# Feed-forward middle tiles: TensorE transposes replaced by VectorE 32x32 block transposes and a trip through DRAM

## The chip, the cores and the metric

The kernel runs on one core of one Trainium2 chip. The metric is the device time of one execution in microseconds (us). The engines are TensorE (PE, with its weight loads as PEld), VectorE (DVE), ScalarE (ACT), GpSimd (POOL) and SyncE (SP), which here issues every DMA.

## The reference

The program is a transformer-like network on a sequence of 256 tokens with 1024 channels: two layers of (feed-forward, mixer, feed-forward), then one mixer, one cross attention and a last feed-forward. There are five feed-forwards, all of one shape. Only they are changed:

```python
def swiglu_ffn(h, w_in, w_out):
    gate, up = jnp.split(h @ w_in, 2, axis=-1)
    return (jax.nn.silu(gate) * up) @ w_out
```

The middle has 2816 channels (`D_FF`), so `w_in` is 1024 x 5632 and `w_out` is 2816 x 1024. All of it is float32.

## The kernel before

The 256 tokens are two tiles of 128 (`t` = 0, 1). Every float32 product is made of three products in a shorter format: an operand is split into a high part (ScalarE's cast to `fp32r`) and a low part (VectorE's difference), and `mac` (L266 to L270) issues high x high (L268), high x low and low x high on TensorE.

Weights stream from DRAM in tiles of 128 x 1024 floats (512 KB) by `wload` (L157 to L166). Each passes three stations. SP loads it into one of `NS` = 5 places of the ring `stage` (L99), ScalarE casts it into one of `NW` = 4 places of `whi` (L164), and VectorE writes the difference into one of 4 places of `wlo` (L165). A load must wait until VectorE has finished with the tile five earlier, a cast until TensorE has finished with the tile four earlier.

`ffn` (L351 to L375) goes over the 2816 middle channels in six chunks, five of 512 and one of 256. A chunk takes four weight tiles for the gate and four for the up half, each tile 12 matmuls; the last chunk has both halves in four tiles. The products come out token-major, tokens on the 128 partitions. For each token tile ScalarE takes the silu (`sg`, L366) and VectorE multiplies it with the up half (`hb`, L368). The second product contracts over the middle channels, so `hb` must be turned: channels on the partitions. `to_T` (L257 to L264) does it with one TensorE transpose per 128 x 128 block, four per token tile, into a PSUM tile `tp` (L262). `split_evac` then reads `tp` twice, once for ScalarE's high part `hTh` (L187) and once for VectorE's low part `hTl` (L188). After the six chunks `lin_out` multiplies `hTh` and `hTl` with 22 tiles of `w_out`, starting with channel block 0.

The order on each engine is set at build time by a scheduler that simulates the program, with priorities: weight loads, casts and differences run ahead of the rest. On the chip each engine then takes its instructions strictly in that order, and so does SP with its DMAs. In the second layer's second feed-forward a preparation of the next block (`s5_prelude`) is put behind chunk 1, and it fills VectorE.

Of the kernel before, what the change touches and what calls it, by code (L numbers as in the profile page):

```python
# [8 lines left out]
F32 = mybir.dt.float32  # L9
# [3 lines left out]
ALU = mybir.AluOpType  # L13
# [3 lines left out]
P = 128  # L17
# [12 lines left out]
ASIDE = 1  # L30
BANKS = dict(mm=7, ch=3, tp=3, chs=4, tpm=2, mmm=3)
BUFS = dict(
    sg=2, hb=2,
    cg=2, xb=2, gv=2, gu=2, sq=2, q=2, k=2, kv=4, xs=2, xd=2, y=2, yo=2, jk=2, pr=2, pT0=2, pT1=2, ao=2, L=2, cbm=2, rp=2,
    D1=2, Mb=2, pm=2, XT=2, X=3, s5m0=2, s5x0=2, s5t=4, sq2=2, tg=1, o2=1, vn=2)
SEQ = "x u q z S A g0 b0 g2 g1 b2 b1"
# [2 lines left out]
LAST = ((0, 512), (512, 256), (768, 256))  # L39
# [13 lines left out]
class Arena:  # L53


    def __init__(self, net, n, name):
        self.t, self.at = net.A([n], name), 0
# [9 lines left out]
class Net:  # L67
    def __init__(self, ctx, tc, a, outs):
        self.tc, self.nc, self.a, self.outs = tc, tc.nc, a, outs
        mk = lambda n, b=None, **k: ctx.enter_context(tc.tile_pool(name=n, bufs=b, **k))  # L70
        self.big = mk("big")
        self.sma, self.small = None, {}
        self.junk = mk("junk", 1)
        self.ps = mk("ps", space=PSUM)
        self.lane = ""
        self.wdma, self.ahead = [], []
        self.sma = Arena(self, 1536, "small")
        self.stage = self.A([NS, 1024], "stage")
        self.whi, self.wlo = [self.A([NW, 1024], n, F32R) for n in ("whi", "wlo")]
        nc = self.nc  # L80
        self.cst = Arena(self, 1024, "cst")
        self.triu = self.load(self.cst, a["c_triu"], [P, P], "triu")
        self.cmask = self.load(self.cst, a["c_cmask"], [P, P], "cmask")
        self.rowm = self.load(self.cst, a["c_rowm"], [P, 4], "rowm")
        self.ones = self.cst.tile([P, P])
        nc.vector.memset(self.ones, 1.0)
        self.mhalf = self.cst.tile([P, 8])
        nc.vector.memset(self.mhalf, -0.5)
        self.euler = self.cst.tile([P, 16])
        nc.vector.memset(self.euler, math.e)  # L90
        self.x = [self.A([D], f"x{t}") for t in range(2)]
# [48 lines left out]
    def mm(self):  # L140
        return self.bank("mm")
# [115 lines left out]
    def to_T(self, src, n, hi, lo, t):  # L257
# [3 lines left out]
        for k in range(n):  # L261
            nc.tensor.transpose(p[:, k * P:(k + 1) * P], src[:, k * P:(k + 1) * P], self.ident)  # L262
        self.split_evac(self._shape(p[:, :n * P], [n, P]),
                        hi[:, :, t * P:(t + 1) * P], lo[:, :, t * P:(t + 1) * P])  # L264

    def mac(self, out, lh, ll, rh, rl, first, last):  # L266
        mm = self.nc.tensor.matmul
        mm(out, lh, rh, start=first, stop=False)  # L268
        mm(out, lh, rl, start=False, stop=False)  # L269
        mm(out, ll, rh, start=False, stop=last)  # L270
# [80 lines left out]
    def ffn(self, norm, w_in, w_out, scale, nxt, aside=None):  # L351
        nc = self.nc
        xT, r = norm["xT"], norm["r"]
        hh, hl = [], []
        for c in range(6):
            n = 512 if c < 5 else 256
            th = self.A([4, S], "hTh", F32R)
            tl = self.A([4, S], "hTl", F32R)
            ps = self.lin_tok(xT, w_in[c * 8:c * 8 + 4], 512)
            if c < 5:  # L360
                pg, pu = ps, self.lin_tok(xT, w_in[c * 8 + 4:c * 8 + 8], 512)
            else:
                pg, pu = [[p[:, i * n:(i + 1) * n] for p in ps] for i in range(2)]
            for t in range(2):
                sg = self.A([512], "sg")
                nc.scalar.activation(sg[:, :n], pg[t][:, :n], AF.Silu, scale=r[t])  # L366
                hb = self.A([512], "hb")
                nc.vector.scalar_tensor_tensor(hb[:, :n], pu[t][:, :n], r[t], sg[:, :n], ALU.mult, ALU.mult)  # L368
                self.to_T(hb, n // P, th[:, :n // P], tl[:, :n // P], t)
            for k in range(n // P):  # L370
                hh.append(th[:, k])
                hl.append(tl[:, k])
            if c == ASIDE and aside:
                aside()
        return self.lin_out((hh, hl), w_out, scale, nxt)  # L375
# [1042 lines left out]
def _tk(w, c0, c1, k0, k1):  # L1418

    b = w[k0 * P:k1 * P, c0:c1].reshape(k1 - k0, P, c1 - c0)  # L1420
    return b.transpose(1, 0, 2).reshape(P, -1)
# [7 lines left out]
def _ffn_in(g, u):  # L1429
    out = []  # L1430
    for c in range(5):
        for w in (g, u):
            for h in range(4):
                out.append(_tk(w, c * 512, c * 512 + 512, h * 2, h * 2 + 2))
    both = np.concatenate([g[:, 2560:], u[:, 2560:]], axis=1)
    return np.stack(out + [_tk(both, 0, 512, h * 2, h * 2 + 2) for h in range(4)])


def _out_w(w, cols=COLS):

    nk = w.shape[0] // P
    if cols is COLS:
        return np.stack([_tk(w, c0, c0 + n, k, k + 2) for c0, n in cols for k in range(0, nk, 2)])
    full = nk // 4 * 4
    o = [_tk(w, c0, c0 + n, k, k + 1024 // n) for c0, n in cols[:2] for k in range(0, nk if n == 512 else full, 1024 // n)]
    if nk > full:
        o.append(np.concatenate([_tk(w, c0, c0 + n, full, nk) for c0, n in cols[1:]], axis=1))
    c0, n = cols[2]
    return np.stack(o + [_tk(w, c0, c0 + n, k, k + 4) for k in range(0, full, 4)])


def _col(g):

    return np.ascontiguousarray(g.reshape(-1, 8, P).transpose(0, 2, 1))


def _prep(inp):
    o = {}
# [5 lines left out]
    for n in ("ffn1", "ffn2"):  # L1464
        o[n + "_norm"] = _col(inp[n + "_norm"])
        w = inp[n + "_w_in"]
        o[n + "_in"] = np.stack([_ffn_in(w[l][:, :FF], w[l][:, FF:]) for l in range(2)])
        o[n + "_out"] = np.stack([_out_w(inp[n + "_w_out"][l]) for l in range(2)])
        o["rope_pos"] = np.ascontiguousarray(inp["positions"].reshape(2, P).T)
    o["rope_freq"] = np.broadcast_to((1.0 / (10000.0 ** (np.arange(0, 32, 2) / 32.0))).astype(np.float32), (P, 16))  # L1470
    w = inp["w_in"]
# [12 lines left out]
    for n, z in (("cq", cqw), ("ckv", ckvw), ("xbc", xbc), ("z", zz), ("uv", uv), ("g", gg), ("uq", uq),  # L1484
                 ("ukv", ukv), ("br", br)):
        o["m1_" + n] = np.stack(z)
    o["m1_out"] = np.stack([_out_w(inp["w_out"][l]) for l in range(2)])
    o["gm_wT"] = inp["gm_w_s"].transpose(0, 3, 1, 2)
    o["gm_b"] = inp["gm_b_s"].transpose(0, 2, 1)
# [7 lines left out]
    c = np.arange(P)  # L1497
# [4 lines left out]
    w = inp["w_in_2"][0]  # L1502
# [27 lines left out]
    o["s5_bglu"] = inp["s5_b_glu_2"][0].reshape(4, P).T  # L1530
    o["s5_glu"] = np.concatenate([_blk(inp["s5_w_glu_2"][0], P * i, P, 4) for i in range(4)])
    o["m2_out"] = _out_w(inp["w_out_2"][0])
    o["mem"] = inp["mem_2"].reshape(2, P, D)
    for k in "qk":
# [1 line left out]
    o["x_v"] = np.concatenate([_blk(inp["w_xv_2"][0], 512 * i, 512, 2) for i in range(2)])  # L1536
    o["x_o"] = _out_w(inp["w_xo_2"][0])
    o["f3_in"] = _ffn_in(inp["w_gate_2"][0], inp["w_up_2"][0])
    o["f3_out"] = _out_w(inp["w_down_2"][0], LAST)
    return o  # L1540


# [31 lines left out]
```

## Time and profile before

| | us |
|---|---|
| median of 3 runs | 1710.42 |
| lowest and highest | 1710.17 to 1711.08 |
| the profiled execution, its own time | 1710.66 |
| its span, first to last instruction | 1708.9 |
| TensorE busy | 1688.4 |
| VectorE busy | 1098.8 |
| ScalarE busy | 911.9 |
| GpSimd busy | 80.1 |

The span is what the profile's windows divide; 1.8 us of the execution lie around it. Matmuls are pipelined, so a matmul's own duration is longer than the distance at which matmuls follow each other: the distance of their starts is what a matmul costs. The granted TensorE clock is the upper of its two levels, 2.4 GHz, in all 40 slices of the page.

### The profile page before, as it was taken

What the parts mean: (1) busy time and instruction counts of PE and PEld (TensorE: products, weight loads), DVE (VectorE), ACT (ScalarE), POOL (GpSimd) and SP (SyncE); (2) the same over time, 40 slices, a digit from 0 to 9 for tenths busy, and PEclk for the clock granted to TensorE, in tenths of its full rate; (3) what the DMA queues carried; (4) which work ended last, traced back from release to release, by engine and by line L of the source; (5) the groups of instructions that cost most, each with busy time, mean ns of one, the idle gap of its engine ahead of it and who ended that gap; (6) DMA issues with size and microseconds to landing.
All of it is one profiled execution on the core that took longest, in us unless ns stands there. A gap on an engine that the chain in (4) does not pass through costs nothing.

```text
span 1708.9 us, 24608 instructions
## 1 busy us (share of the span) xinstructions
PE 1688.4 (99%) x9442; PEld 1447.1 (85%) x9442; DVE 1098.8 (64%) x1780; ACT 911.9 (53%) x1361; POOL 80.1 (5%) x73
## 2 busy tenths in 40 slices
PE   8999999999999999999999999999999999999998
PEld 6888898888888888888988888888899888888888
DVE  5555598657555555555896666798589746655554
ACT  5444466564554445444666545545476556555443
POOL 0000013000000000000130000000010100000000
PEclk9999999999999999999999999999999999999999
DMA  7556555444555555556654446655664124346552
GB/s 251 186 185 204 177 192 187 160 140 137 198 192 185 185 174 196 185 188 190 201 189 149 164 137 197 195 176 163 206 198 137 63 65 164 108 160 196 197 188 96
DMA packets 89543, 293.07 MB, mean 172 GB/s; under 512 B 14672, under 2 KB 15952, under 8 KB 89424
## 3 DMA queue, kind: packets, MB, share of 16 engines
q1 hardware_dynamic: 89424, 291.49, 52.1%
q8 instruction: 74, 1.21, 0.3%
q14 instruction: 45, 0.37, 0.1%
HBM read 290.41 MB, written 1.05 MB: 171 GB/s over the span
## 4 chain that ended last, share of the span: by engine, by line
PE 96%; DVE 2%; ACT 1%; issue 0%; DMA 0%; POOL 0%; SPq 0%; POOLq 0%; DVEq 0%
PE mm L269 28%; PE mm L268 28%; PE mm L270 28%; PE tp L262 2%; PE tp L205 1%; PE mmm L268 1%; PE mmm L270 1%; PE mmm L269 1%; PE ch L734 1%; PE chs L981 1%; PE ch L756 1%; DVE wlo L165 0%; PE ch L1119 0%; PE tp L618 0%; PE ch L697 0%
## 5 line engine op out<-in xcount | busy, mean ns | idle before, releaser
L165 DVE TENSOR_TENSOR wlo<-stage,whi 128x1024 fp32r<-128x1024 f32 (+3 forms) x552 | 661.8, 1202 | 465.6 <-ACT whi L164 464.0
L164 ACT CAST whi<-stage 128x1024 fp32r<-128x1024 f32 (+3 forms) x552 | 570.9, 1036 | 581.7 <-PE mm L270 475.2
L269 PE MATMUL mm<-wlo,xh 128*128 128x512 f32 (+3 forms) x1264 | 485.6, 386 | 0.0
L270 PE MATMUL mm<-whi,xl 128*128 128x512 f32 (+4 forms) x1264 | 481.5, 386 | 0.0
L268 PE MATMUL mm<-whi,xh 128*128 128x512 f32 (+3 forms) x1264 | 476.3, 387 | 0.1
L268 PEld LDWEIGHTS mm<-whi,xh 128*128 128x128 f32 x1264 | 237.4, 188 | 45.4 <-ACT xh L209 0.5
L269 PEld LDWEIGHTS mm<-wlo,xh 128*128 128x128 f32 x1264 | 237.9, 188 | 44.5
L270 PEld LDWEIGHTS mm<-whi,xl 128*128 128x128 f32 x1264 | 236.8, 188 | 44.7
L268 PE MATMUL mm<-whi,hTh 128*128 128x512 f32 (+1 forms) x484 | 179.7, 372 | 0.0
L270 PE MATMUL mm<-whi,hTl 128*128 128x512 f32 (+1 forms) x484 | 179.5, 371 | 0.0
L269 PE MATMUL mm<-wlo,hTh 128*128 128x512 f32 (+1 forms) x484 | 179.2, 370 | 0.0
L173 POOL TENSOR_TENSOR small<-small,cst 128x1 f32<-128x1 f32 (+2 forms) x60 | 60.4, 1013 | 1170.2 <-DVE small L171 1158.1
L270 PEld LDWEIGHTS mm<-whi,hTl 128*128 128x128 f32 x484 | 91.2, 188 | 15.3
L269 PEld LDWEIGHTS mm<-wlo,hTh 128*128 128x128 f32 x484 | 91.3, 189 | 15.2
L268 PEld LDWEIGHTS mm<-whi,hTh 128*128 128x128 f32 x484 | 91.3, 189 | 15.1
L269 PE MATMUL mm<-xl,whi 128*128 128x256 f32 x320 | 90.8, 284 | 1.1 <-DVE xl L210 1.1
L268 PE MATMUL mm<-xh,whi 128*128 128x256 f32 x320 | 90.8, 285 | 1.0 <-ACT xh L209 1.0
L270 PE MATMUL mm<-xh,wlo 128*128 128x256 f32 x320 | 89.9, 283 | 0.0
L269 PEld LDWEIGHTS mm<-xl,whi 128*128 128x128 f32 x320 | 61.3, 192 | 1.6 <-DVE xl L210 1.5
L268 PEld LDWEIGHTS mm<-xh,whi 128*128 128x128 f32 x320 | 61.1, 191 | 1.3 <-ACT xh L209 1.3
L270 PEld LDWEIGHTS mm<-xh,wlo 128*128 128x128 f32 x320 | 61.1, 192 | 0.0
L187 ACT CAST hTh<-tp 128x512 fp32r<-128x512 f32 (+1 forms) x60 | 30.8, 553 | 41.9 <-PE tp L262 41.8
(526 smaller groups left out, 2007.5 us busy)
## 6 DMA issues: line engine op xcount, KB each, us to landing
stage<-in_ffn_in SPq DMA_DIRECT2D x176, 512.0 KB, 3.5
stage<-in_ffn_out SPq DMA_DIRECT2D x88, 512.0 KB, 3.5
stage<-in_m_g SPq DMA_DIRECT2D x48, 512.0 KB, 4.3
stage<-in_f_in SPq DMA_DIRECT2D x44, 512.0 KB, 3.3
stage<-in_m_br SPq DMA_DIRECT2D x24, 512.0 KB, 3.7
stage<-in_m_out SPq DMA_DIRECT2D x24, 512.0 KB, 3.6
stage<-in_f_out SPq DMA_DIRECT2D x22, 512.0 KB, 3.2
stage<-in_m_xbc SPq DMA_DIRECT2D x16, 512.0 KB, 4.4
```

Of the source, the lines that this page charges most:

```text
L164: nc.scalar.copy(h, s)
L165: self.wsub = nc.vector.tensor_tensor(l, s, h.bitcast(F32), ALU.subtract).ins
L173: nc.gpsimd.tensor_tensor(r, m, self.mhalf[:, :n], ALU.pow)
L187: self.nc.scalar.copy(hi, ps)
L205: nc.tensor.transpose(p[:, k, t * P:(t + 1) * P], x[t][:, (k0 + k) * P:(k0 + k + 1) * P], self.ident)
L262: nc.tensor.transpose(p[:, k * P:(k + 1) * P], src[:, k * P:(k + 1) * P], self.ident)
L268: mm(out, lh, rh, start=first, stop=False)
L269: mm(out, lh, rl, start=False, stop=False)
L270: mm(out, ll, rh, start=False, stop=last)
L734: pe.matmul(p3[:, i], qT[:96, b * hb + i, toks[t]], kT[:96, b * hb + i, :nk], start=True, stop=True)
L756: pe.matmul(p[:, h * 64:(h + 1) * 64], pT[kb][:, h], vv[kb][:, h], start=kb == 0, stop=kb == t)
L981: pe.matmul(q, self.s5bc[ct][:, 2 * (E5 - 1 - e) + i], um[:, :, e], start=e == 0, stop=e == E5 - 1)
```

## The change

A method `flip` takes the place of `to_T` in `ffn`. VectorE's 32x32 block transpose turns every 32 x 32 block of `hb` in its own place (`flip`, 128 x 512 in SBUF). What is left to do is to move whole blocks between partitions, and that is done by DMA: four stores, one for each group of 32 partitions, write the tile into a DRAM tile of 128 x 512 in runs of 128 floats, and one load brings it back (`flipped`, rows of 512 floats). `split_evac` then reads `flipped` from SBUF. The rows come back in an order in which channel (within a chunk) is not k x 128 + p, and so the rows of `w_out` are permuted on the host by `_flipped`. The last chunk does the same with 256 channels, in runs of 64 floats.

```diff
-    sg=2, hb=2,
+    sg=2, hb=1, flip=2, flipped=1,
...
+        self.dram = mk("dram", 2, space=bass.MemoryType.DRAM)
...
+    def flip(self, src, n, hi, lo, t):
+        nc = self.nc
+        w = n * 32
+        r = self.A([512], "flip")[:, :4 * w]
+        nc.vector.transpose(r, src)
+        d = self.dram.tile([P, 4 * w], F32, name="flips", tag="flips")
+        to = d.rearrange("(j c) (i e) -> i c j e", c=32, e=w)
+        for i in range(4):
+            nc.sync.dma_start(out=to[i], in_=r[i * 32:i * 32 + 32].rearrange("p (j e) -> p j e", e=w))
+        raw = self.A([512], "flipped")[:, :4 * w]
+        nc.sync.dma_start(out=raw, in_=d)
+        tok = slice(t * P, (t + 1) * P)
+        hi, lo = [z[:, :, tok].rearrange("p k (a b) -> p k a b", b=32) for z in (hi, lo)]
+        self.split_evac(raw.rearrange("p (a k b) -> p k a b", k=n, b=32), hi, lo)
...
-                hb = self.A([512], "hb")
-                nc.vector.scalar_tensor_tensor(hb[:, :n], pu[t][:, :n], r[t], sg[:, :n], ALU.mult, ALU.mult)
-                self.to_T(hb, n // P, th[:, :n // P], tl[:, :n // P], t)
+                hb = self.A([512], "hb")[:, :n]
+                nc.vector.scalar_tensor_tensor(hb, pu[t][:, :n], r[t], sg[:, :n], ALU.mult, ALU.mult)
+                self.flip(hb, n // P, th[:, :n // P], tl[:, :n // P], t)
...
+def _flipped(w):
+    o = [w[c0:c0 + n * P].reshape(4, n, 32, -1).transpose(1, 0, 2, 3).reshape(n * P, -1)
+         for c0, n in [(c * 512, 4) for c in range(5)] + [(2560, 2)]]
+    return np.concatenate(o)
...
-        o[n + "_out"] = np.stack([_out_w(inp[n + "_w_out"][l]) for l in range(2)])
+        o[n + "_out"] = np.stack([_out_w(_flipped(inp[n + "_w_out"][l])) for l in range(2)])
...
-    o["f3_out"] = _out_w(inp["w_down_2"][0], LAST)
+    o["f3_out"] = _out_w(_flipped(inp["w_down_2"][0]), LAST)
```

On TensorE's list the 220 transposes are gone, and the other instructions stand in the same order, but for the stretch of `s5_prelude` and a few neighbouring matmuls in the feed-forwards that change places. On the other engines new instructions are set between old ones. The same code stands 1 to 25 lines lower in the changed file, so the line numbers differ.

SP in the first feed-forward, from the loads of chunk 0 on. Before, nothing but weight loads (`stage`), 28 in a row:

```order
L99 DMA cst<-in_rope_freq 128x16
L99 DMA stage<-in_ffn_in 128x1024 x28
L99 DMA small<-in_mix_norm 128x8
L99 DMA stage<-in_ffn_in 128x1024 x7
```

Of the change (`flips` is the DRAM tile, L277 the stores, L279 the load):

```order
L100 DMA stage<-in_ffn_in 128x1024 x7
L277 DMA flips<-flip 32x4x128 x4
L100 DMA stage<-in_ffn_in 128x1024
L277 DMA flips<-flip 32x4x128
L279 DMA flipped<-flips 128x512
L277 DMA flips<-flip 32x4x128 x3
L100 DMA stage<-in_ffn_in 128x1024 x2
L279 DMA flipped<-flips 128x512
L100 DMA stage<-in_ffn_in 128x1024 x5
```

Ten DMAs per chunk now stand between its eight weight loads. The load of token tile 0 stands behind the first store of token tile 1, and three stores and two weight loads stand behind it.

ScalarE at the end of chunk 0 and into chunk 1 (`whi` is a weight cast, `hTh` the high part of the turned tile). Before:

```order
L393 ACTIVATE cst<-small 128x32
L164 CAST whi<-stage 128x1024 x4
L187 CAST hTh<-tp 128x4x128 x2
L164 CAST whi<-stage 128x1024 x2
L366 ACTIVATE sg<-mm,small 128x512
```

Of the change:

```order
L165 CAST whi<-stage 128x1024 x5
L188 CAST hTh<-flipped 128x4x128
L165 CAST whi<-stage 128x1024
L384 ACTIVATE sg<-mm,small 128x512
L165 CAST whi<-stage 128x1024
L384 ACTIVATE sg<-mm,small 128x512
L188 CAST hTh<-flipped 128x4x128
L165 CAST whi<-stage 128x1024 x6
```

The two casts of `hTh` stood side by side; now the first stands one weight cast later and the second another two later, behind both silus of the next chunk's gate.

VectorE at the same place (`hb` is the product, `hTl` the low part). Before:

```order
L368 SCALAR_TENSOR_TENSOR hb<-mm,small,sg 128x512 x2
L165 TENSOR_TENSOR wlo<-stage,whi 128x1024 x2
L188 TENSOR_TENSOR hTl<-tp,hTh 128x4x128 x2
L165 TENSOR_TENSOR wlo<-stage,whi 128x1024 x6
```

Of the change:

```order
L386 SCALAR_TENSOR_TENSOR hb<-mm,small,sg 128x512
L273 STREAM_TRANSPOSE flip<-hb 128x512
L166 TENSOR_TENSOR wlo<-stage,whi 128x1024
L386 SCALAR_TENSOR_TENSOR hb<-mm,small,sg 128x512
L273 STREAM_TRANSPOSE flip<-hb 128x512
L166 TENSOR_TENSOR wlo<-stage,whi 128x1024 x2
L189 TENSOR_TENSOR hTl<-flipped,hTh 128x4x128
L166 TENSOR_TENSOR wlo<-stage,whi 128x1024 x2
L189 TENSOR_TENSOR hTl<-flipped,hTh 128x4x128
```

Between a block transpose and the `hTl` of its tile stand three weight differences for token tile 0 and four for token tile 1.

## Rows read from the trace of the kernel before

**Rows 1.** The page: TensorE's row, its granted clock in 40 slices, the chain by engine.
```profile
PE 1688.4 (99%) x9442; PEld 1447.1 (85%) x9442; DVE 1098.8 (64%) x1780; ACT 911.9 (53%) x1361; POOL 80.1 (5%) x73
...
PEclk9999999999999999999999999999999999999999
...
PE 96%; DVE 2%; ACT 1%; issue 0%; DMA 0%; POOL 0%; SPq 0%; POOLq 0%; DVEq 0%
```
**Rows 2.** Chain that ended last, in order of time: start us, us, what.
```profile
38.64 0.87 PE tp L262 x8
61.33 0.87 PE tp L262 x8
...
129.30 0.87 PE tp L262 x8
```
**Rows 3.** Instructions of the tile hb: durations min/median/max in ns.
```profile
L262 PE MATMUL tp<-cst,hb x220: 270/272/328, 38.5 to 1646.8; 128*128 128x128 f32 x110
```
**Rows 4.** Timeline of TensorE, chunk 0: start us, us, engine line op.
```profile
28.27 0.39 PE L268 MATMUL mm<-whi,xh 128*128 128x512 f32 x1
...
37.79 0.39 PE L268 MATMUL mm<-whi,xh 128*128 128x512 f32 x1
```
**Rows 5.** Who waited for whom: us in total, times, longest us.
```profile
ACT whi L164 <- PE mm L270: 475.2, 335, 4.8
...
SPq L99 <- DVE wlo L165: 1180.7, 459, 12.7
```
**Rows 6.** Timeline of VectorE, end of chunk 0.
```profile
33.46 1.40 DVE L368 SCALAR_TENSOR_TENSOR hb<-mm,small,sg 128x512 f32<-128x512 f32 x2
35.04 1.22 DVE L165 TENSOR_TENSOR wlo<-stage,whi 128x1024 fp32r<-128x1024 f32 x1 [0.18 <-ACT whi L164]
```
**Rows 7.** Timeline of VectorE, a 128x512 operation from SBUF to SBUF.
```profile
1163.06 0.69 DVE L919 TENSOR_TENSOR s5k<-lays 128x512 f32<-128x512 f32 x1
```
**Rows 8.** Instructions of the tensor in_c_stril: SP's time for one issue, in ns.
```profile
L99 SPq DMA_DIRECT2D lay<-in_c_stril x1: 430/430/430, 1203.3 to 1203.3; - x1
```
**Rows 9.** DMA view, issues: xcount, KB each, median us to landing.
```profile
stage<-in_ffn_in SPq DMA_DIRECT2D x176, 512.0 KB, 3.5
...
stage<-in_s_glu SPq DMA_DIRECT2D x4, 256.0 KB, 2.6
out<-fo SPq DMA_DIRECT2D x4, 256.0 KB, 2.3
lay<-in_gm_wT SPq DMA_DIRECT2D x2, 256.0 KB, 4.4
...
lay<-in_ssd_norm SPq DMA_DIRECT2D x2, 256.0 KB, 6.1
...
cst<-in_c_ident SPq DMA_DIRECT2D x1, 64.0 KB, 1.9
...
cst<-in_c_triu SPq DMA_DIRECT2D x1, 64.0 KB, 8.2
...
lay<-in_c_stril SPq DMA_DIRECT2D x1, 64.0 KB, 5.3
```
**Rows 10.** Timeline of ScalarE, end of chunk 0 and chunk 1.
```profile
36.63 1.06 ACT L164 CAST whi<-stage 128x1024 fp32r<-128x1024 f32 x1 [1.62 <-PE mm L270]
39.11 1.08 ACT L187 CAST hTh<-tp 128x512 fp32r<-128x512 f32 x2 [1.43 <-PE tp L262]
40.25 1.05 ACT L164 CAST whi<-stage 128x1024 fp32r<-128x1024 f32 x1
...
46.68 0.68 ACT L366 ACTIVATE sg<-mm,small 128x512 f32<-128x512 f32 x1
48.44 1.06 ACT L164 CAST whi<-stage 128x1024 fp32r<-128x1024 f32 x1 [1.08 <-PE mm L270]
```
**Rows 11.** Windows: busy us (and count) of each engine, PEclk, DMA share, GB/s.
```profile
455.00:560.00 105.00, 105.00 (x485) 87.35 (x485) 59.43 (x58) 50.76 (x58) 0.00 (x0) 1.00 0.58 189
...
1110.00:1120.00 10.00, 10.00 (x45) 8.26 (x45) 10.00 (x23) 3.63 (x4) 0.00 (x0) 1.00 0.57 189
```
**Rows 12.** DMA queues: packets, MB, share of 16 engines.
```profile
q1 hardware_dynamic: 89424, 291.49, 52.1%
```

## The prediction

> **What bounds the kernel now.** The page comes first. TensorE is busy for 99% of the span, its clock stands at the upper level in every slice, and 96% of the chain that ended last is TensorE's own work [rows 1]. So the time is a sum of matmul distances, and time that is taken off TensorE's list comes off the end, as long as nothing else makes TensorE wait. The chain in order of time shows what the transposes weigh: one group of eight per chunk, 0.87 us each, at 38.64, 61.33 and so on to 129.30 us [rows 2]. There are 220 transposes of `hb` in all [rows 3].
>
> Then the waits, to see how far the other engines are from being late. ScalarE's casts waited 335 times, 475 us in all, for a matmul, and SP's loads 459 times for a weight difference [rows 5]. Both run ahead until their rings are full, so they have time to spare. How much is worked out below, because the new DMAs will use it.
>
> **What the change removes.** In chunk 0 matmuls of 512 columns start at 28.27 and, 42 starts later, at 37.79 us [rows 4], which is 0.2267 us each. A tile of 12 takes 2.72 us and a chunk of eight tiles 21.76 us. Groups of transposes stand (129.30 - 38.64) / 4 = 22.67 us apart [rows 2], so a group costs 22.67 - 21.76 = 0.91 us, or 0.113 us for one transpose. 220 of them are **24.9 us**. The low end is the chain's own 0.87 us for eight, 23.9 us. ScalarE and VectorE still make `hTh` and `hTl`, from SBUF and no longer from PSUM; I count them as equal.
>
> The Trainium skill ("TensorE: Matmul & The Clock Gate", Wait — 56ns, not 53.3ns?) gives 55.8 ns between matmuls of 128 columns at the full clock. By it the 220 would be worth only 12.3 us, and the time would be about 1700 us. The trace differs: 0.87 us for eight is 109 ns each [rows 2]. The distance is measured here at the full clock, so the page's figure gets no chance of its own and the sum above stays.
>
> **What it adds, beside other work.** Sixty block transposes on VectorE. No row shows one. A 128x512 operation of VectorE from SBUF to SBUF took 0.69 us [rows 7] and a 128x1024 one 1.22 us [rows 6]; those are the bounds, and I take 0.69, the same number of elements. Two per chunk are 1.4 us in a chunk in which VectorE is busy for 59.43 of 105 us [rows 11]. That is hidden by its idle time, except behind chunk 1 of the second layer's second feed-forward, where it is busy for 10.00 of 10 us [rows 11].
>
> SP issues ten more DMAs per chunk, at 0.43 us each [rows 8]: 4.3 us of 21.76, while it mostly waits. The DMA engines carry 8 x 512 KB per chunk now, at 189 GB/s and a busy share of 0.58 [rows 11]. The stores and loads add 4 x 256 KB = 1.05 MB per chunk. By bytes the share goes to about 0.58 x 22.67 / 21.76 x 1.25 = 0.76: no bound. Do runs of 512 bytes cost more? All packets took 52.1% of 16 x 1708.9 us [rows 12], 14,245 us. About 70,700 of them are the weights' 4 KB rows (552 loads of 128), and at 0.58 x 16 x 105 us for 4845 such packets (189 GB/s times 105 us) they take 0.20 us each, or 14,200 us. That leaves almost nothing for the other 18,700 packets, most of them short. So I count by bytes.
>
> **What it adds on the path: a round trip.** `hTh` now waits for a block transpose, stores, their landing, a load and its landing, and behind `hTh` on ScalarE stand weight casts. On VectorE weight differences stand behind `hTl`, and on SP weight loads stand behind `flipped`. So the question is whether the trip ends before those are missed.
>
> The spare time: a cast starts when the tile four earlier is done on TensorE, and TensorE reaches its tile three tiles later, after 8.16 us. Cast and difference take 1.06 + 1.22 us [rows 6, 10]. A cast may start **5.9 us** late.
>
> Landing of a store is bounded by 1.9 us (64 KB in runs of 512 bytes, into an idle queue) and 8.2 us (64 KB behind the first weight loads); between them lie 2.3 us (the output, the only stores there are) and 5.3 us (64 KB in a burst of small loads). A load of 256 KB lands after 2.6 to 6.1 us, 4.4 us in the midst of weight loads [rows 9]. I take 2.3 and 4.4, the nearest in kind and in place.
>
> Token tile 0 of chunk 0: `hb` starts at 33.46 us and takes 0.70, so the block transpose ends at 34.8. Four issues and 2.3 us of landing lead to 38.5, the load to 42.9. ScalarE comes to this `hTh` after the cast that was at 40.25 us, now 0.9 earlier, so at 40.4 [rows 10]. It waits 2.5 us, and the next cast, due at 42.1, starts at 43.5, **1.4 us late of 5.9**. Token tile 1: the other three stores go out behind the first load, until 39.9, land at 42.2, and the second load at 46.6. ScalarE comes to it after the second silu, at 46.68 + 0.68 - 0.9 = 46.5 [rows 10]. No wait. Then six casts without a visitor bring the ring back, as ScalarE and VectorE are busy for little more than half of a chunk [rows 11]. TensorE notices nothing. The last chunk's tiles are needed some ten weight tiles, 27 us, later.
>
> **The sum.** Against the profiled execution's own 1710.66 us: minus 24.9, plus 1.0 us where VectorE is full (ten block transposes of 0.69 us are 6.9, of which the spare 5.9 us hide the rest) = 1686.8 us. That execution lies 0.24 us above the median of the runs shown, so I forecast **1687 us** for a median, in whole microseconds. With the low price of a TensorE transpose it would be 1687.6, with no loss at all 1685.5.
>
> **Rivals.**
> *The trip is too long (slower).* Place: the cast behind the second `hTh` of each chunk on ScalarE. It hangs on three landings in a row, store, store, load. The point: if each is 2.1 us above what I took, the second `hTh` ends at 53.5 us, and the cast due at 48.44 - 0.9 = 47.5 [rows 10] is 5.9 us late. Every further us of a landing costs 3 us in each of 25 chunks. At 5.3 us for each store and 6.1 us for the load [rows 9] the three are 7.7 us longer, of which 5.9 plus the 0.3 us to spare are covered: 1.5 us x 25 = 37 us lost against 24.9 won, about **1722 us**. With 8.2 us for a store it would be far above 1850. For it: a store here is 128 short runs, and weight loads share the queue. Against: those slow rows stand behind a backlog that steady chunks don't have, where weights land in 3.5 us [rows 9]. The Trainium skill ("VectorE: DVE Perf Modes", The three transpose paths) warns that a plain DMA copy that transposes by strides is 19 times slower when the innermost stride at the destination is large. Here the innermost runs are 512 bytes long on both sides, so the rule speaks for this rival only as far as the DRAM writes are short; no row of this trace shows such a copy.
>
> *VectorE becomes the bound behind the preparation.* Where it is busy for 10.00 of 10 us [rows 11] the ten flips come with 6.9 us of block transposes, and every wait of an `hTl` for its trip is lost for good, as there is no idle time to catch up. With 1.5 us each, between the 2.5 us and none of the two tiles above: 10 x 0.69 + 10 x 1.5 - 5.9 = 16 us lost, so about **1702 us**. Against: the differences between a transpose and its `hTl` stand there as before, and the preparation can slide into the next tiles.
>
> *No change.* The DMA queues become the bound. If a 512-byte run cost as much as a 4 KB row, 0.20 us, stores would add 1024 x 0.20 / 16 = 12.8 us to a chunk's 12.8 us of weights and 3.2 us of loads: 28.8 us against 21.76, or 175 us more. With costs between, the gain is just eaten at a chunk of 22.67 us: **1710 us**. The packet sum speaks against it.
>
> That the change does not do what it says is excluded: the 220 transposes are gone from TensorE's list.
>
> **How the numbers follow.** A measurement of this kernel tells about 0.2%, 3.4 us, from no change. The forecast has 0.73, VectorE as the bound 0.08, no change 0.05, the long trip 0.14. Faster is the forecast and the VectorE case, 0.81; the same 0.05; slower 0.14. The range begins at 1683, which leaves room for dearer transposes (a few idle moments that follow them go too), and ends at 1704 to take in the VectorE case. It leaves out the no-change and the slow case, 0.19.
>
> **What would show it.** Right: matmul starts of 21.76 us per chunk without a break, no `tp` of `hb` in the chain, still 96% TensorE, casts waiting for matmuls and a few us per chunk for `flipped`. A store should land in about 2 to 3 us, a load in about 4. Wrong: if the chain goes through DMA and `hTh` in each chunk, or TensorE shows idle time before the matmuls that use the casts behind `hTh`, the trip is too long; if DMA share stands near 0.9 in the feed-forwards with weights landing in over 6 us, the queues bind.

## The result, and the profile after

The changed kernel took 1685.56 us (median of four runs, 1682.59 to 1686.97), against 1710.3 us for the kernel before beside it (1708.25 to 1711.08). The ratio is 0.9855, with an interval of 0.9838 to 0.9872: **faster by about 25 us**, 1.4 us below the forecast of 1687. The profiled execution took 1684.61 us, its span is 1682.7 us. Four more runs, later, gave a median of 1684.11 us.

The page of the changed kernel: the engines' busy time, TensorE's granted clock in 40 slices, the queue that carries nearly all DMAs, the chain by engine.

```profile
PE 1662.7 (99%) x9222; PEld 1423.0 (85%) x9222; DVE 1133.0 (67%) x1840; ACT 902.6 (54%) x1361; POOL 78.6 (5%) x73
...
PEclk9999999999999999999999999999999999999999
...
q1 hardware_dynamic: 132624, 320.35, 60.7%
...
PE 96%; DVE 1%; ACT 1%; issue 0%; DMA 0%; POOL 0%; SPq 0%; POOLq 0%; DVEq 0%; ACTq 0%
```

TensorE has 220 instructions fewer than in [rows 1], is still busy for 99% of a span that is 26.2 us shorter, and still makes up 96% of the chain. The bound is the same; its list is shorter. Within the first feed-forward the chain (30 to 135 us, by line) holds nothing but matmuls, where [rows 2] had a group of transposes every 22.67 us:

```profile
by line: PE mm L288 33.5%; PE mm L287 33.4%; PE mm L286 33.3%
```

The waits: who waited for whom, us in total, times, longest; SP's own queue in the last rows.

```profile
ACT whi L165 <- PE mm L288: 351.3, 240, 4.8
...
ACT hTh L188 <- DMA flipped<-flips: 148.5, 56, 7.3
...
DVE hTl L189 <- ACT hTh L188: 99.6, 54, 4.2
...
SPq L100 <- DVE wlo L166: 889.6, 387, 11.8
SPq L279 <- DMA flips<-flip: 100.6, 87, 4.2
```

Against [rows 5], ScalarE's casts wait 124 us less for matmuls, and 148.5 us for the trip's load instead: the idle time of an engine that ran ahead has paid for the trip. SP gave up 291 us of its waits for weight differences in the same way. The longest wait for the load, 7.3 us, lies in the fourth feed-forward (before the `hTh` at 1118.08 us); TensorE was busy there for 31.00 of 31 us (1099 to 1130).

The DMA view (issues: xcount, KB each, median us to landing) and the window of one feed-forward, which answers to [rows 11]:

```profile
stage<-in_ffn_in SPq DMA_DIRECT2D x176, 512.0 KB, 4.3
...
flips<-flip SPq DMA_DIRECT2D x200, 64.0 KB, 3.4
flipped<-flips SPq DMA_DIRECT2D x50, 256.0 KB, 3.7
```
```profile
455.00:560.00 105.00, 105.00 (x465) 86.95 (x464) 68.80 (x74) 51.66 (x60) 0.00 (x0) 1.00 0.79 248
```

The end of chunk 0 on ScalarE and on SP (timelines: start us, us, engine line op; in brackets the idle time before and its releaser):

```profile
39.90 1.05 ACT L165 CAST whi<-stage 128x1024 fp32r<-128x1024 f32 x1 [1.66 <-PE mm L288]
43.06 0.62 ACT L188 CAST hTh<-flipped 128x512 fp32r<-128x512 f32 x1 [2.10 <-DMA flipped<-flips]
43.58 1.05 ACT L165 CAST whi<-stage 128x1024 fp32r<-128x1024 f32 x1
...
45.34 1.06 ACT L165 CAST whi<-stage 128x1024 fp32r<-128x1024 f32 x1
...
49.77 0.62 ACT L188 CAST hTh<-flipped 128x512 fp32r<-128x512 f32 x1 [2.80 <-DMA flipped<-flips]
50.30 2.00 ACT L165 CAST whi<-stage 128x1024 fp32r<-128x1024 f32 x2
```
```profile
35.53 1.83 SPq L277 DMA_DIRECT2D flips<-flip  x4
...
39.37 0.34 SPq L279 DMA_DIRECT2D flipped<-flips  x1
39.76 1.73 SPq L277 DMA_DIRECT2D flips<-flip  x3
41.53 1.06 SPq L100 DMA_DIRECT2D stage<-in_ffn_in  x2
44.43 0.33 SPq L279 DMA_DIRECT2D flipped<-flips  x1
```

A reader measures how late a cast is from the last one that waited for a matmul (39.90), in steps of a tile, 2.72 us: 42.62, 45.34, 48.06. The casts came at 43.58, 45.34 and 50.30, so 1.0, 0 and 2.2 us late. That is inside the spare 5.9 us, and TensorE did not wait.

### The profile page after: what moved, and what is told of

Read it like the earlier page. It is cut to its first block, busy times and chain, and to the rows that moved or that the text cites. A ratio compares the mean times of both kernels' runs of the same rounds, so it can differ in the third digit from the quotient of the medians.

```text
span 1682.7 us, 24668 instructions
## 1 busy us (share of the span) xinstructions
PE 1662.7 (99%) x9222; PEld 1423.0 (85%) x9222; DVE 1133.0 (67%) x1840; ACT 902.6 (54%) x1361; POOL 78.6 (5%) x73
## 3 DMA queue, kind: packets, MB, share of 16 engines
q1 hardware_dynamic: 132624, 320.35, 60.7%
## 4 chain that ended last, share of the span: by engine, by line
PE 96%; DVE 1%; ACT 1%; issue 0%; DMA 0%; POOL 0%; SPq 0%; POOLq 0%; DVEq 0%; ACTq 0%
PE mm L287 28%; PE mm L286 28%; PE mm L288 28%; PE tp L206 1%; PE mmm L286 1%; PE mmm L288 1%; PE mmm L287 1%; PE ch L752 1%; PE chs L999 1%; PE ch L774 1%; PE tp L263 1%; PE ch L1137 0%; PE tp L636 0%; PE ch L715 0%; ACT whi L165 0%
## 5 line engine op out<-in xcount | busy, mean ns | idle before, releaser
L188 ACT CAST hTh<-flipped 128x512 fp32r<-128x512 f32 (+1 forms) x60 | 35.1, 585 | 160.0 <-DMA flipped<-flips 148.5
L189 DVE TENSOR_TENSOR hTl<-flipped,hTh 128x512 fp32r<-128x512 f32 (+1 forms) x60 | 38.8, 647 | 99.6 <-ACT hTh L188 99.6
```

The costliest lines, as they stand in the source:

```text
L188: self.nc.scalar.copy(hi, ps)
L189: self.nc.vector.tensor_tensor(lo, ps, hi.bitcast(F32), ALU.subtract)
```

## The experiments

The theory: 220 transposes of 0.113 us came off a list that sets the time, and everything that was added lies in the idle time of engines that run ahead. The rivals: the trip or VectorE costs something that the gain hides; or the gain has another source. In each diff lines with - are those of the changed kernel, except where the text says otherwise; ... marks what is left out. The kernel before ran beside each of the three sets of experiments, with medians of 1710.41, 1710.53 and 1710.54 us, so times of different sets can be compared.

**1. The trip left out.**

```diff
...
-        d = self.dram.tile([P, 4 * w], F32, name="flips", tag="flips")
...
-        nc.sync.dma_start(out=raw, in_=d)
+        raw = r
```

> The block transposes stay, the stores and loads through DRAM are left out: hTh and hTl are made from the block-transposed tile itself, so the blocks stand in the wrong places and the output is not the reference's. Theory (the round trip is hidden in the 5.9 us that a weight cast may be late): no change against the changed kernel, 1685.6 us within 3 us, though ScalarE no longer waits for the load. Rival (the trip takes a part of the gain back, by waits or by contention on the DMA queues): 1680 us or less.

Measured: 1684.84 us (1683.77 to 1685.28), ratio to before 0.9848 [0.9834, 0.9863]. That is 0.7 us below the first four runs of the change and 0.7 us above the four later ones. The trip through DRAM costs nothing that can be measured.

**2. Nothing turned at all** (as in 1, and `raw = src` without the block transpose).

> Neither block transposes nor stores and loads: hTh and hTl are made from hb as it stands, so nothing is turned and the output is not the reference's. This is the floor, with all work on the middle tiles' turning taken away. Theory: 1684.6 us within 3 us, at most the 1.0 us below the changed kernel that I charged where VectorE is full. Rival (VectorE is the bound behind the preparation): about 7 to 16 us below the changed kernel, 1670 to 1679 us.

Measured: 1684.04 us (1682.62 to 1685.25), ratio 0.9844 [0.983, 0.9859]. This is the floor: the same program with all work on the turning left out, under the same scheduler. The change stands at it, within 1.5 us. Its sixty block transposes are as good as free.

**3. The change, with TensorE's transposes kept beside it** (into a PSUM tile that nobody reads).

```diff
+        p = self.tp()
+        for k in range(n):
+            nc.tensor.transpose(p[:, k * P:(k + 1) * P], src[:, k * P:(k + 1) * P], self.ident)
```

> The changed kernel with the 220 TensorE transposes put back beside the new path; nobody reads what they write. Theory (the gain is the length of TensorE's list): 1685.6 + 24.9 = 1710.5 us within 4 us. Rival (the gain comes from elsewhere: PSUM banks that come free, the two reads of PSUM, the waits of hTh for TensorE): 1686 to 1698 us.

Measured: 1722.37 us (1721.14 to 1723.12), ratio 1.0068 [1.0053, 1.0083], 12 us above what was expected. Most of the miss sits in one place. After the first feed-forwards this kernel stands where the kernel before stood (the transposes of `x` that follow the second one are at 597.23 us on TensorE's timeline, against 597.13), and before the fourth it is 0.6 us behind (1054.34 against 1053.78). So far the length of TensorE's list accounts for the whole gain: the reads of `tp` for `hTh` and `hTl` are gone in this kernel too, and it is no faster for it. After the fourth, the one with the preparation of the next block behind chunk 1, it is 9.7 us behind (1225.74 against 1216.02). Its windows there, two of 10 us (the busy times are PE, PEld, DVE, ACT, POOL; then PEclk), and TensorE's timeline:

```profile
1150.00:1160.00 10.00, 5.98 (x31) 4.71 (x30) 10.00 (x27) 3.19 (x6) 0.00 (x0) 0.89 0.60 177
1160.00:1170.00 10.00, 9.17 (x35) 6.90 (x33) 10.00 (x34) 1.94 (x6) 0.00 (x0) 0.77 0.25 93
```
```profile
1155.36 0.43 PE L978 MATMUL tp<-cst,s5b 128*128 128x128 f32 x2 [0.74 <-DVE s5b L836]
1159.07 1.54 PE L978 MATMUL tp<-cst,s5b 128*128 128x128 f32 x6 [3.29 <-DVE s5b L839]
```

VectorE is full, and TensorE waits for it, 3.29 us at once. The granted clock is 0.89 in the window in which TensorE is busy for 5.98 of 10 us, and 0.77 in the next, so for a part of the time at the lower level of 1.2 GHz. The rival "VectorE becomes the bound" exists in this kernel, in the stretch where the prediction placed it. What TensorE waits for is not `hb` but `s5b`, a tile of the preparation, and the changed kernel has the same transposes of `s5b` on TensorE's list. There VectorE is busy for 10.00 of 10 us too, in three windows from 1130 to 1160 us, and TensorE for 29.99 of 30. The two kernels' work is set differently in that stretch: the first transpose of `s5b` comes 99 us after the transposes of `x` that precede the fourth feed-forward in the changed kernel, and 92 us here. Whether that is why the changed kernel escapes was not tried.

**4. TensorE's transposes doubled in the kernel before** (- and + against that kernel; only where `ffn` calls it).

```diff
...
-        for k in range(n):
+        for k in range(2 * n if self.twice else n):
+            k = k % n
...
+                self.twice = True
...
```

> The kernel before with every transpose of hb done twice into the same place, 440 instead of 220. Theory (0.113 us of TensorE's list for each): 1710.3 + 24.9 = 1735.2 us within 4 us. Rival (0.0558 us each, as 128 columns at the full clock): 1722.6 us. If they lay in time that TensorE has to spare: 1710 us.

Measured: 1734.36 us (1734.16 to 1734.69), ratio 1.0139 [1.0123, 1.0156]. That is 23.95 us above its 1710.41 us, 0.109 us for each of the 220. The chain of this kernel, first two chunks:

```profile
38.09 1.75 PE tp L263 x16
61.62 1.75 PE tp L263 x16
```

The groups stand 23.53 us apart, 0.86 us more than in [rows 2]. A transpose of 128 columns that is added costs the end 0.109 us; what one that is taken away gives back follows below.

**5. Two trips** (a second store and load of 256 KB behind the first).

```diff
...
         nc.sync.dma_start(out=raw, in_=d)
+        d = self.dram.tile([P, 4 * w], F32, name="again", tag="again")
+        nc.sync.dma_start(out=d, in_=raw)
+        raw = self.A([512], "second")[:, :4 * w]
+        nc.sync.dma_start(out=raw, in_=d)
...
```

> The changed kernel with a second trip behind the first: the turned tile is stored to DRAM again and loaded again, one store and one load of 256 KB more per token tile. The scheduler, which knows of the trip, sets hTh later on ScalarE and VectorE (the first one behind both silus of the next chunk). Theory (the trip is hidden as long as its end stands near its place in the order, and 5.9 us catch the rest): the feed-forwards keep 21.76 us per chunk, only the stretch with VectorE full loses up to 10 us, 1686 to 1696 us. Rival 1 (the trip is hidden by a fixed 5.9 us): in the changed kernel the second cast behind the trips was 2.2 us late; 7.4 us more (3.7 for a store and for a load) leave 2.2 + 7.4 - 5.9 = 3.7 us per chunk, 25 x 3.7 = 93 us, 1778 us. Rival 2 (the DMA queues bind): per chunk 4.2 + 2.1 MB in 21.76 us are 289 GB/s, where 251 GB/s took a share of 0.80: a share of 0.92, just not bound, but weights would land after 6 us and more.

Measured: 1762.7 us (1761.1 to 1769.76), ratio 1.0304 [1.0287, 1.0321], 77 us above the change. The two extra landings are 2.6 and 3.7 us. The theory's own number was wrong here: this is the rival in which the trip is too long, on the chip. The chain by engine, and the second `hTh` of chunk 0 and both of chunk 1 on ScalarE:

```profile
PE 57%; DMA 29%; DVE 6%; issue 3%; SPq 2%; ACT 2%; POOL 0%; POOLq 0%; ACTq 0%; DVEq 0%
...
57.29 0.62 ACT L188 CAST hTh<-second 128x512 fp32r<-128x512 f32 x1 [4.06 <-DMA second<-again]
...
77.46 0.62 ACT L188 CAST hTh<-second 128x512 fp32r<-128x512 f32 x1 [7.05 <-DMA second<-again]
...
84.81 0.62 ACT L188 CAST hTh<-second 128x512 fp32r<-128x512 f32 x1 [4.82 <-DMA second<-again]
```

DMAs, 0% of the chain of the change, are 29% of this one. The share of the DMA engines is 0.72 in its window 455 to 560, less than in the changed kernel: the engines are not what binds.

**6. One landing more** (a copy from SBUF to SBUF behind the load), to find the edge between 1 and 5.

```diff
...
         nc.sync.dma_start(out=raw, in_=d)
+        one = raw
+        raw = self.A([512], "second")[:, :4 * w]
+        nc.sync.dma_start(out=raw, in_=one)
...
```

> One more DMA behind the load, from SBUF to SBUF, so that each trip is one landing longer. The theory says that a longer trip costs nothing until the second hTh of a chunk is 5.9 us late, and everything from there on. In the changed kernel the cast behind it was 2.2 us late, which leaves 3.7 us. The two extra landings of the doubled trip, 2.6 and 3.7 us, made the second hTh 7.5 us later (57.29 against 49.77 us), 3.8 us over the edge, 95 us for 25 chunks, against some 77 to 85 measured. One landing of 2.6 us should then make it about 3.1 us later, still under the edge: 1685 to 1690 us. Rival: there is no edge, and each us of trip costs its share, 77 us x 2.6 / 6.3 = 32 us: about 1717 us.

Measured: 1712.3 us (median of ten runs, 1704.73 to 1715.84), ratio 1.0009 [0.9995, 1.0022]; the copy lands after 2.5 us. The changed kernel beside it took 1684.11 us (1683.81 to 1684.51). So 2.5 us per trip cost 28 us. Both guesses missed, the one without an edge by less. But the trace has an edge; what was wrong is how lateness was taken to end. The first `hTh` of chunks 0 to 3 on ScalarE, in chunk 2 with the casts around it and in chunk 3 with the one behind it:

```profile
48.06 0.62 ACT L188 CAST hTh<-second 128x512 fp32r<-128x512 f32 x1 [2.46 <-DMA second<-flipped]
...
70.83 0.62 ACT L188 CAST hTh<-second 128x512 fp32r<-128x512 f32 x1 [3.46 <-DMA second<-flipped]
...
87.07 1.05 ACT L165 CAST whi<-stage 128x1024 fp32r<-128x1024 f32 x1 [1.67 <-PE mm L291]
...
95.66 0.62 ACT L188 CAST hTh<-second 128x512 fp32r<-128x512 f32 x1 [6.53 <-DMA second<-flipped]
96.18 1.05 ACT L165 CAST whi<-stage 128x1024 fp32r<-128x1024 f32 x1
...
118.50 0.62 ACT L188 CAST hTh<-second 128x512 fp32r<-128x512 f32 x1 [6.92 <-DMA second<-flipped]
119.03 1.05 ACT L165 CAST whi<-stage 128x1024 fp32r<-128x1024 f32 x1
```

Behind chunk 2 the next cast was due at 87.07 + 2.72 = 89.79 and came at 96.18, 6.4 us late; behind chunk 3, where the last cast that waited for a matmul started at 109.53, it was due at 112.25 and came at 119.03, 6.8 us late. TensorE idled 0.4 us between 80 and 100 us and 0.8 us between 120 and 140 us, and not at all between 40 and 80 us, where no cast was that late. So the edge near 5.9 us is there. But the wait grows from chunk to chunk, 2.5, 3.5, 6.5, 6.9 us. VectorE's timeline at the start of the trips of chunks 1 and 2 shows why:

```profile
57.89 0.74 DVE L389 SCALAR_TENSOR_TENSOR hb<-mm,small,sg 128x512 f32<-128x512 f32 x1
...
78.09 0.69 DVE L189 TENSOR_TENSOR hTl<-second,hTh 128x512 fp32r<-128x512 f32 x1 [2.90 <-ACT hTh L188]
79.04 2.36 DVE L166 TENSOR_TENSOR wlo<-stage,whi 128x1024 fp32r<-128x1024 f32 x2 [0.25 <-DMA stage<-in_ffn_in]
81.31 0.74 DVE L389 SCALAR_TENSOR_TENSOR hb<-mm,small,sg 128x512 f32<-128x512 f32 x1
```

The `hb` of chunk 2 starts 23.42 us after that of chunk 1, not 21.76. In its list it stands behind two weight differences, and these behind the `hTl` of the chunk before, which waited for its trip. A late trip makes the next trip start later. In the changed kernel the first waits of chunks 0 to 4 are 2.1, 2.1, 2.7, 2.5 and 2.2 us: there it does not grow.

Not all of the loss is idle time of TensorE. The profiled span is 30.2 us longer than that of the change (1712.9 against 1682.7); TensorE idles for 18.2 us more of it and is busy for 12.0 us longer (1674.7 against 1662.7) with the same 9222 instructions. In experiment 5 it is 51.4 and 33.9 us of 85.3. The granted clock has a part in that: it is 0.91 in some stretches of 20 us around such idle time (580 to 600 us here, 540 to 560 in experiment 5), and 1.00 in the change; where it is low in experiment 3, matmuls of 512 columns start 0.43 us apart (1161.30 to 1162.58 us) and not 0.2267. How large that part is was not separated.

**7. Two trips, issued by GpSimd**, so that no weight load stands behind them on SP (`nc.gpsimd.dma_start` in place of `nc.sync.dma_start`, in `flip` of experiment 5).

> The doubled trip, with all its DMAs issued from GpSimd's queue, so that no weight load stands behind them on SP's list. It tells what cost the 77 us of the doubled trip. The theory: hTh is late on ScalarE, and the casts behind it; the trip is as long from the other queue, so most of the loss stays: 1745 to 1775 us. Rival: weight loads were held up on SP behind the trip's issues (SP waited 147 us for the first load and 91 us for the second store), and without them the loss goes: 1686 to 1695 us.

Measured: 1762.26 us (1758.4 to 1768.96), ratio 1.031 [1.0288, 1.0333]: the same as with SP. SP waits for hardly anything but weight differences now (1227.4 us, against 717.0 in experiment 5), and TensorE waits for `hTh` itself:

```profile
SPq L100 <- DVE wlo L166: 1227.4, 459, 12.7
```
```profile
PE mm L290 <- ACT hTh L188: 26.7, 12, 5.9
```

So held-up weight loads are not needed for the loss. It is no clean separation, though: by this queue the four landings are longer, 4.2, 5.1, 3.9 and 4.3 us against 3.4, 3.9, 2.6 and 3.7, so a part of the loss may have changed its cause.

**8. One trip, issued by GpSimd.**

> The changed kernel with the stores and loads of the trip issued from GpSimd's queue, so that no weight load stands behind one on SP. Theory (SP's waits are covered by the ring of five): 1685.6 us within 3 us; the waits of SP for flips go, ScalarE's waits for the load stay in the order of 150 us. Rival (weight loads behind the trip cost part of the gain): 1 to 3 us faster. If GpSimd's issues take longer than SP's 0.43 us, the trip gets longer and the stretch with VectorE full loses some us.

Measured: 1688.09 us (1687.65 to 1688.79), ratio 0.9871 [0.9857, 0.9886]. The trip is now out of ScalarE's way, though it is no shorter (stores land after 3.8 us, loads after 4.7): the scheduler has set both `hTh` behind both silus, and in chunk 0 neither waits:

```profile
46.34 0.61 ACT L188 CAST hTh<-flipped 128x512 fp32r<-128x512 f32 x1
...
51.20 0.62 ACT L188 CAST hTh<-flipped 128x512 fp32r<-128x512 f32 x1
...
1677.91 0.72 ACT L1429 ACTIVATE fo<-fo,small 128x512 f32<-128x512 f32 x1 [1.11 <-POOL small L174]
```

And nothing comes of it, since there was nothing to gain. The last activation starts at 1677.91 us, against 1678.52 in the changed kernel, yet the span ends at 1685.9 against 1682.7: 8.0 us after it, where the changed kernel needs 4.2 us. The 2.5 us lost stand behind all work.

**9. Two buffers each for `hb` and `flipped`**, twice.

```diff
-    sg=2, hb=1, flip=2, flipped=1,
+    sg=2, hb=2, flip=2, flipped=2,
```

> The changed kernel with two buffers for hb and for flipped, as hb had before. Theory (buffers play no part: the order on VectorE frees hb before it is written again, and the second load waits for its stores, not for flipped): 1685.6 us within 2.5 us. Rival (the single flipped holds back the second load of each chunk and with it ScalarE): 1 to 3 us faster, and shorter waits of hTh.

Measured: 1682.06 us (1681.73 to 1685.15), ratio 0.984 [0.9825, 0.9854]. That looked like 3.5 us, so it was done again beside the changed kernel.

> Two buffers each for hb and flipped, once more, beside the changed kernel on the same chip. The theory: they free at most the 1 us that the change loses where VectorE is full; the rest of the 3.5 us between the medians was the start of the span (the first waits for x) and chance: 0 to 1.5 us below the changed kernel of this call, intervals that overlap. Rival: the trips of a chunk overlap better and that is worth 3 us or more again, with intervals that do not overlap.

> The changed kernel once more, as the base for the three runs beside it. Both theories: 1683 to 1687 us, as measured before (1682.59 to 1686.97).

Measured: 1684.96 us (1682.2 to 1686.4) with the buffers, 1684.11 us (1683.81 to 1684.51) without. There is no difference. The transposes of `x` that follow the first feed-forward stand at 165.63 and 167.29 us in the two profiles with the buffers, at 167.03 and 166.41 us in the two without: by so much the start of the span, with its wait for the input, varies from one execution to the next.

**10. More of the same:** two more tensors of the mixer, `yaT` and `ycT`, turned by `flip`, which takes 32 further transposes from TensorE (the rows of their branch weights are permuted on the host).

```diff
...
-                self.to_T(u, 4, yaT[0], yaT[1], t)
+                self.flip(u, 4, yaT[0], yaT[1], t)
...
-                self.to_T(y, 4, ycT[0], ycT[1], t)
+                self.flip(y, 4, ycT[0], ycT[1], t)
...
```

> The changed kernel with 32 more transposes moved from TensorE to the trip: the two tiles of the gated branch and the two of the scan branch in both mixers, whose turned form is needed 40 us later; the rows of their branch weights are permuted on the host. Theory (TensorE's list is the time here too): 32 x 0.113 = 3.6 us less than the changed kernel, 1682 us within 2.5 us. Rival (in the mixers the casts behind the trip make TensorE wait, since VectorE is busy for 37 of 40 us where the first of them stands): 1686 us or more.

Measured: 1689.45 us (1688.83 to 1691.31), ratio 0.9881 [0.9866, 0.9895]: slower than the change. Of the 1.8 us that 16 transposes are worth in each of the two mixers, next to nothing arrives (the second one, from the end of the third feed-forward to the start of the fourth, takes 270.19 us against 270.34). A new wait stands there, TensorE for the merged heads:

```profile
PE mm L286 <- ACT mh L188: 2.9, 4, 0.8
```

The larger loss is elsewhere: from the end of the fourth feed-forward to the start of the fifth (1196.57 to 1495.07 us) the time is 298.5 us, against 294.0 and 295.5 in the two profiles of the changed kernel, in code that the edit doesn't touch. The scheduler has put that work in another order; which instruction makes the 3 to 4.5 us was not found out.

## Why the prediction was right

**The gain.** The transposes of `x` that follow a feed-forward show in the chain how far the program has come. After the first, second and fourth feed-forward and before the fifth, in the kernel before:

```profile
171.50 0.88 PE tp L205 x8
...
597.13 0.88 PE tp L205 x8
...
1216.02 0.87 PE tp L205 x8
...
1511.09 0.87 PE tp L205 x8
```

And in the changed kernel:

```profile
167.03 0.87 PE tp L206 x8
...
587.67 0.88 PE tp L206 x8
...
1196.53 0.87 PE tp L206 x8
...
1490.56 0.87 PE tp L206 x8
```

After the third they stand at 783.43 and 768.99. The differences after the four are 4.47, 9.46, 14.44 and 19.49: about 5.0 us for each feed-forward, or 0.113 us for each of its 44 transposes, the forecast's price; experiment 4 gives 0.109, its low end. The last feed-forward adds 5.7 us, of which 0.7 lie behind all work (from the start of the last activation to the end of the span it is 4.18 us, before 4.85). Between the fourth and the fifth another 1.0 us goes, but not by the change: the profile of the later runs took 295.45 us there, against 295.07 before and 294.03 in the first profile, and its granted clock from 1440 to 1500 us is 0.97, as in the kernel before, where the first profile has 1.00. Against the 12.3 us that one would estimate for all 220 from the 55.8 ns of the Trainium skill ("TensorE: Matmul & The Clock Gate", Wait — 56ns, not 53.3ns?), experiment 4 measured 23.95 us: for these transposes of float32 tiles the page's figure does not hold, and the distance read from the chain does.

**The block transposes.** Taken at 0.69 us, bounded by 0.69 and 1.22; measured 0.71 us (timeline of VectorE, `flip`). VectorE's busy time in the window rose from 59.43 to 68.80 of 105 us, which its idle time took in; experiments 1 and 2 differ by 0.8 us, and their ranges overlap.

**The DMA engines.** Forecast a share of 0.76 by bytes, measured 0.79. The 43,200 added packets took 60.7% x 16 x 1682.7 - 52.1% x 16 x 1708.9 = 2,100 us, 0.05 us each, against 0.20 us for a 4 KB row in the prediction: far from the rival in which a short run costs as much as a long one, but half as much again as bytes alone would give (28.86 MB on top of 291.49 MB in 14,245 us are 1,410 us). Weight loads land in 4.3 us instead of 3.5.

**The trip.** For tile 0 the forecast was good: from `hb` to the landed load 9.4 us, measured 9.05 us (34.01 to 43.06), and ScalarE waited 2.1 us where 2.5 were forecast. For tile 1 it was not: forecast no wait, measured 2.8. The step that failed is the sum that put its landed load at 46.6 us; it came at 49.77. SP had issued the last store by 41.5 us and not by 39.9, the load behind it went out at 44.43 and not at 42.2, and it took 5.3 us and not 4.4; of the 3.1 us in all, 0.6 are the later start of `hb` (34.01 against 33.46). That made a cast 2.2 us late, against 5.9 to spare, so it did not show in the time.

**VectorE where it is full.** Forecast 1.0 us lost. From the transposes of `x` ahead of it to those behind it, the fourth feed-forward with its preparation took 162.24 us before (1053.78 to 1216.02) and 157.20 us in the first profile of the change (1039.33 to 1196.53), so 5.0 us less: the whole price of its 44 transposes. In the profile of the later runs it took 156.25 us, 6.0 us less. So against the kernel before the term was nothing once and a gain of 1.0 us once. Against the floor (156.21 us with nothing turned, experiment 2) 1.0 us was lost once and nothing once.

**What was right by luck.** "Six casts without a visitor bring the ring back" holds for the changed kernel and was taken as a rule. Experiment 6 shows that it is a condition: with 2.5 us more per trip the next trip starts late as well. The rival of the long trip was priced by a single chunk, with 6.2 us covered in its row of landings (store, store, load). If what is added to both trips of a chunk lies in that row, 2 x 2.5 = 5.0 us more should have cost nothing, and 28 us were measured, the whole gain; the doubled trip with 2 x 6.3 = 12.6 us should have cost 6.4 x 25 = 160 us, and 77 us were measured. So the loss begins earlier than by that price, and by this estimate rises more slowly. Why it rises more slowly stays open; one thing that the traces show is that the scheduler gave way. In experiment 6 it set both `hTh` of chunk 0 one weight cast later: the second came 4.2 us later than in the change (54.01 against 49.77), but the cast behind it, due at 43.55 + 3 x 2.72 = 51.71, came at 54.53, 2.8 us late, where the change has 2.2. The Trainium skill ("VectorE: DVE Perf Modes", The three transpose paths) warns of a plain copy that transposes by strides, 19 times slower than the crossbar's transpose when the innermost stride at the destination is large. Here the innermost runs are 512 bytes long, so its case did not arise: a 64 KB store landed in 3.4 us, against 2.6 us for a 256 KB store in long rows (experiment 5).

## What to carry to other kernels

Where one engine is busy for 99% and is the chain, price what leaves its list by the distance in the chain, and then ask of everything added only whether it ends within the time by which the other engines run ahead; going to the floor (experiment 2) tells when to stop. Lateness in a loop is safe only if an iteration's late result does not stand ahead of the next iteration's start on an in-order engine: look at two iterations, not at one. And do not read a change in a kernel with a scheduler as local: experiment 10 lost 3 to 4.5 us in a stage that it didn't touch.

## What was not expected of the hardware

- DMAs issued by GpSimd lengthen the end of the execution: 8.0 us from the start of the last activation to the end of the span with one trip per tile (experiment 8), against 4.1 to 4.9 us in the twelve profiles in which SP issues all. With two trips (experiment 7) it is 9.2 us, 1757.84 to 1767.0. What the span waits for there was not seen.
- A landing depends little on the size here: 2.5 us for 256 KB from SBUF to SBUF, 2.6 us for a 256 KB store in rows of 2 KB, 3.4 us for 64 KB in runs of 512 bytes, 3.7 us for a 256 KB load, all amid weight loads.
- By GpSimd's queue the same trips were cut into 12,160 packets, not 43,200, yet landed later (experiment 8): stores after 3.8 us and loads after 4.7 us.
